# The sample's attention begun beside the prompt's output projection, in an encoder trunk of two batches on one core

## The chip, the cores and the metric

One core of a Trainium2 chip runs the whole program. Its engines are TensorE (PE, matrix products), VectorE (DVE), ScalarE (ACT), GpSimd (POOL) and SyncE (SP), which here issues nearly all transfers (DMAs). Each engine works through its own queue in order. The metric is the device time of one execution in microseconds, the median of several.

## The reference

A hybrid encoder layer is run for two batches with the same weights: `x_prompt` (512 rows) and `x_sample` (1024 rows), width 1024, all in float32.

```python
h = _rmsnorm(x, norm_attn_g)
z = h @ w_in                       # q 512 | k 128 | v 128 | ca 512 | cb 512
a_out = _window_attn(q, k, v, bias, band, attn_sink)   # 8 heads of 64, 2 kv heads, |q-k| <= 128
c = ca * jax.nn.sigmoid(cb)
c = _dwconv(c, conv_dw_w, conv_dw_b)                   # depthwise, 31 taps along the rows
c = jax.nn.silu(_layernorm(c, conv_ln_g, conv_ln_b))
x = x + jnp.concatenate([a_out, c], axis=-1) @ w_out
h = _rmsnorm(x, norm_ffn_g)
u = _dwconv(h @ w_up, ffn_dw_w, ffn_dw_b)              # 3 taps, 2 x 2816 channels
x = x + (jax.nn.silu(u[..., :D_FF]) * u[..., D_FF:]) @ w_down
return _rmsnorm(x, norm_final_g)
```

The attention scores get a bias per head from a table of relative positions (`bias`), and a sink logit per head.

## The kernel before

A product of two float32 matrices is made of three passes: each operand is split into a rounded part and the rest (`hi`, `lo`), and hi x hi, hi x lo and lo x hi are added up. `split` makes the parts: ACT rounds (L150), POOL or DVE subtracts (L151). One matmul is 128x128 weights by 512 columns.

The program goes in stages, in the order in which the code is written:

- **Projection A.** `order` lists the 14 column chunks of `w_in`. Each is split, multiplied (`proj`, L277 to L279) and evacuated (`evac`). The first four chunks are done for all three row tiles (the prompt, and two halves of the sample), the other ten for the prompt alone: `cs[0..3]` (the convolution's gates, cb and ca), `kv_`, then `qs` (four query chunks). Queries go to DRAM (`qsd`, L360) and come back per block (L551). The bias table is spread into DRAM (`bbd`), and `load_bias` fetches one 128x384 tile a head (L536).
- **Projection B beside the prompt's attention.** The ten chunks left for the sample: `kv_`, `cs[2]`, `qs`, `cs[3]`. Sample keys and values go to DRAM (`ksd` L377, `vsd` L393). At each `tick` in the projection, generators advance by a number of steps: `side` holds `prompt()`, that is, attention of 8 units (a unit is one block of 128 rows and one kv head) with the convolution's normalization (`conv_norm`: L675, L677 to L681, L687) for the last four.
- **Output projection of the prompt** (`out_half`, L711 to L713, weights L737 and L739), then `make_h2`, which scales the rows (L762, by the sum of squares that L723 makes) and transposes them (L237, L239, L240).
- **FFN of the prompt**, 22 steps (`ffn_step`): up projection, three taps (L846), gate (L864 to L869), down projection every second step (L884 to L887). Beside it runs `sample()`, from step `U0` = 3: attention of the sample's 16 units, loading and splitting of `w_out`, and two convolution norms. Keys, values and bias for it are loaded by `load_kv` (L749, L753) and a second `load_bias` just ahead.
- **The sample's output projection and FFN** (from L1039 on), which is ordered by hand and not touched.

A unit of attention: scores (`scores`, L574) into a PSUM bank, DVE adds the bias and takes the maximum (L578), ACT takes the exponential (L587), DVE the reciprocal (L589), ACT, DVE or POOL scale (L593, L595). Then transposes (L616), split (L618, L619), products with the values (L630, L631), evacuation (L638 to L642).

The depthwise convolution (`conv_items`) is not matrix work: 23 or 26 taps of a tile are multiply-adds on DVE (L313 first, L317 the others, accumulating in a PSUM bank, L325 last), 7 or 4 are products on ACT (L306, L309) added on POOL (L310). `convs` holds the prompt's four channel groups, `late` the sample's four. `pace` sets how much of each goes by at a tick: `rate` for `side`, `conv` for `convs`, `late` for `late` once `convs` is empty.

These steps give a written order only. A scheduler takes the instructions from it and fixes each engine's queue, and slots in SBUF (`sb`: 15 `q` of 4 KB, 61 `h` of 2 KB and others) and PSUM banks decide when a tile can be had; `use` says which banks a job may take.

## Time and profile before

| | |
|---|---|
| median of 3 runs | 1554.61 us (1553.9 to 1559.92) |
| profiled execution | 1557.32 us, its span 1555.2 us |
| TensorE (PE) | busy 1500.7 us, 96%, 6800 matmuls in the record |
| VectorE (DVE) | busy 1186.8 us, 76% |
| ScalarE (ACT) | busy 801.5 us, 52% |
| GpSimd (POOL) | busy 738.0 us, 47% |
| first score of the prompt | at 138 us |
| first output projection of the prompt | at 297 us |
| first transposing for its FFN | at 349 us |
| last down projection of the prompt | at 818 us |
| mean granted clock of TensorE | 0.987 |

The profile's page gives busy times, the span in 40 slices, and groups of instructions by line and engine. Its other views give busy times by stretch, with the granted clock of TensorE; the waits, each with the instruction that ended it (`PE a L574 <- DVE s L578: 6.5, 1, 6.5` says that the matmul of line 574 into a tile `a` waited for line 578 on DVE, 6.5 us in all, once, 6.5 at the longest); and the instructions in order of time. In the names of groups, `out<-in` are tiles by kind of slot (`h`, `q`, `c`, `d`; `a`, `b`, `c`, `u` are PSUM banks), and the two numbers behind the bar are the busy time and the mean ns of one. A queue's own entries are marked by a q (SPq).

### The profile page before, as it was taken

How to read it: one execution, taken by the hardware profiler on the slowest of the kernel's cores; microseconds unless marked ns; L12 is line 12 of the kernel's file. 1: busy time of each engine (PE TensorE's matmuls, PEld its weight loads, DVE VectorE, ACT ScalarE, POOL GpSimd, SP SyncE). 2: the span in 40 equal slices, each digit the busy share in tenths (PEclk: the TensorE clock that was granted, in tenths of full speed). 3: DMA queues.
4: the chain of work that ended last, by engine and by line, in shares of the span. 5: the costliest groups of instructions: out<-in, count | busy, mean ns of one | idle time of the engine just before them, and what ended most of it. 6: DMA issues, size and time to landing. Idle time of an engine off the chain costs nothing. (4 is left out here: it accounts for less than half of the span.)

```text
span 1555.2 us, 20044 instructions
## 1 busy us (share of the span) xinstructions
PE 1500.7 (96%) x6800; PEld 1232.1 (79%) x6800; DVE 1186.8 (76%) x1669; ACT 801.5 (52%) x1414; POOL 738.0 (47%) x648
## 2 busy tenths in 40 slices
PE   8998899897999999999999999999999999999997
PEld 7886688686877887888878888888888888788886
DVE  7787958656978899666665777877787877877795
ACT  7432654634566665555554454455444555544364
POOL 3464256226577776656562333555555554000135
PEclk9999899999999999999999999999999999999999
DMA  9435324634333333323547122332232232694642
GB/s 376 151 118 152 97 75 123 207 129 132 96 127 95 95 96 109 122 89 109 190 158 266 57 95 75 102 102 102 102 102 102 106 111 90 212 362 146 218 144 108
DMA packets 109441, 211.80 MB, mean 136 GB/s; under 512 B 11635, under 2 KB 33267, under 8 KB 109212
## 3 DMA queue, kind: packets, MB, share of 16 engines
q1 hardware_dynamic: 108092, 209.46, 40.4%
q8 instruction: 53, 0.87, 0.2%
q10 hardware_dynamic: 1248, 1.09, 0.2%
q14 instruction: 48, 0.39, 0.1%
HBM read 163.03 MB, written 48.51 MB: 136 GB/s over the span
## 5 line engine op out<-in xcount | busy, mean ns | idle before, releaser
L151 POOL TENSOR_TENSOR q<-q,q 128x1024 fp32r<-128x1024 f32 x66 | 159.0, 2412 | 88.7 <-ACT q L150 37.9
L992 POOL TENSOR_TENSOR q<-q,q 128x512 fp32r<-128x512 f32 x82 | 115.5, 1421 | 153.8 <-ACT q L1101 149.9
L277 PE MATMUL u<-h,q 128*128 128x512 f32 x384 | 151.4, 396 | 1.1 <-DVE h L846 0.7
L278 PE MATMUL u<-h,q 128*128 128x512 f32 x384 | 152.1, 396 | 0.0
L279 PE MATMUL u<-h,q 128*128 128x512 f32 x384 | 150.9, 393 | 0.0
L1115 PE MATMUL w<-h,q 128*128 128x512 f32 x372 | 146.2, 393 | 2.7 <-ACT h L1196 1.7
L1117 PE MATMUL w<-h,q 128*128 128x512 f32 x372 | 145.0, 390 | 0.7 <-POOL q L992 0.7
L317 DVE SCALAR_TENSOR_TENSOR c<-c,cvw,c 128x512 f32<-128x512 f32 x184 | 137.9, 750 | 2.5
L1116 PE MATMUL w<-h,q 128*128 128x512 f32 x350 | 136.2, 389 | 0.0
L150 ACT CAST q<-q 128x1024 fp32r<-128x1024 f32 x66 | 69.0, 1047 | 82.7 <-POOL q L151 39.9
L989 POOL TENSOR_TENSOR q<-q,q 128x1024 f32<-128x1024 f32 x8 | 23.8, 2994 | 180.7 <-DVE q L989 169.5
L1424 PE MATMUL w<-h,h 128*128 128x512 f32 x264 | 102.7, 389 | 0.0
L1426 PE MATMUL w<-h,h 128*128 128x512 f32 x264 | 102.7, 389 | 0.0
L992 DVE TENSOR_TENSOR h<-h,h 128x512 fp32r<-128x512 f32 (+1 forms) x128 | 92.2, 763 | 11.4 <-ACT h L996 9.5
L1425 PE MATMUL w<-h,h 128*128 128x512 f32 x244 | 94.9, 389 | 0.0
L992 POOL TENSOR_TENSOR c<-q,c 128x512 fp32r<-128x512 f32 x46 | 72.6, 1590 | 43.9 <-ACT c L1101 43.9
L996 ACT CAST h<-h 128x512 fp32r<-128x512 f32 x101 | 58.7, 619 | 58.4 <-DVE h L992 29.6
L1115 PEld LDWEIGHTS w<-h,q 128*128 128x128 f32 x372 | 69.8, 188 | 20.4 <-ACT w L1187 3.3
L277 PEld LDWEIGHTS u<-h,q 128*128 128x128 f32 x384 | 72.8, 190 | 16.3 <-DVE h L846 1.3
L279 PEld LDWEIGHTS u<-h,q 128*128 128x128 f32 x384 | 72.7, 189 | 14.2
L278 PEld LDWEIGHTS u<-h,q 128*128 128x128 f32 x384 | 72.7, 189 | 13.7
L1117 PEld LDWEIGHTS w<-h,q 128*128 128x128 f32 x372 | 69.8, 188 | 15.8 <-POOL q L992 1.1
(472 smaller groups left out, 4372.5 us busy)
## 6 DMA issues: line engine op xcount, KB each, us to landing
q<-in_laid_w_up SPq DMA_DIRECT2D x88, 512.0 KB, 3.6
h<-in_w_down SPq DMA_DIRECT2D x90, 256.0 KB, 4.2
ga<-q SPq DMA_DIRECT2D x64, 256.0 KB, 2.0
h<-ga SPq DMA_DIRECT2D x57, 256.0 KB, 3.8
q<-in_laid_w_in SPq DMA_DIRECT2D x22, 512.0 KB, 4.5
q<-in_x_sample SPq DMA_DIRECT2D x15, 512.0 KB, 7.6
h<-qsd SPq DMA_DIRECT2D x24, 256.0 KB, 3.1
q<-ga SPq DMA_DIRECT2D x20, 256.0 KB, 4.4
```

The lines of the kernel that those rows point to most:

```text
L151: (nc.vector if dve else nc.gpsimd).tensor_tensor(lo[:], raw[:], hi[:].bitcast(F32), op=ALU.subtract)
L277: nc.tensor.matmul(out, whi[:, kc, :], hi[:], start=(kc == 0), stop=False)
L278: nc.tensor.matmul(out, whi[:, kc, :], lo[:], start=False, stop=False)
L279: nc.tensor.matmul(out, wlo[:, kc, :], hi[:], start=False, stop=(kc == KC - 1))
L317: nc.vector.scalar_tensor_tensor(acc[:], src(t), w(t), acc[:], op0=ALU.mult, op1=ALU.add)
L992: (eng or nc.vector).tensor_tensor(out, a, b, op=ALU.subtract)
L1115: nc.tensor.matmul(out, whi[:, s], hi[:], start=(start and c == 0), stop=False, **go)
L1116: nc.tensor.matmul(out, whi[:, s], lo[:], start=False, stop=False, **go)
L1117: nc.tensor.matmul(out, wlo[:, s], hi[:], start=False, stop=(stop and c == 3), **go)
L1424: nc.tensor.matmul(out, sh[:, c], th[:], start=(p == 0), stop=False)
L1425: nc.tensor.matmul(out, sh[:, c], tl[:], start=False, stop=False)
L1426: nc.tensor.matmul(out, sl[:, c], th[:], start=False, stop=(p == NPAIR - 1))
```

## The change

The code moves work; it adds no computation, and TensorE's matmuls are the same in number.

- In projection A the prompt's keys, values and queries come right after `cs[0]` and `cs[1]`, and `cs[2]`, `cs[3]` last. Projection B has the order `kv_`, `qs`, `cs[2]`, `cs[3]`.
- The bias tiles for the prompt are loaded after chunk `BL` = 9 (the last queries), two heads to a slot of 4 KB (`q`), and not after projection A.
- The sample's convolution gets no share at the ticks of both projections (`late=0`). Once a tile of a convolution is begun it is finished before another queue goes on (`mid`).
- When the prompt's last scores are made (its bias list is empty), the sample's keys, values and bias are loaded, and the generator of its attention takes one step for each `SA` = 4 steps of the prompt's rest, output projection and `make_h2`. The rest of it runs in the FFN from step 0 instead of 3, at 0.44 steps a tick instead of 0.52; the loading of `w_out` for the sample waits for step `KW` = 21. Transposing in `make_h2` may use the banks `a` and `b`, before `a` alone.

```diff
-RA, RB, RBO, RD, RN, RE = 1.2, 0.8, 2.5, 0.52, 0.8, 0.9
+RA, RB, RBO, RD, RN, RE = 1.2, 0.8, 2.5, 0.44, 0.8, 0.9
-CL, CLO, CD = 0.5, 0.6, 0.65
+CLO, CD = 0.6, 0.65
-U0 = 3
+BL = 9
+SA = 4
+KW = 21
...
-    order = cs[0] + cs[1] + cs[2] + cs[3] + kv_ + qs
+    order = cs[0] + cs[1] + kv_ + qs + cs[2] + cs[3]
-    order += kv_ + cs[2] + qs + cs[3]
+    order += kv_ + qs + cs[2] + cs[3]
...
-        queue = convs or (late if pace["late"] else convs)
-        while queue and pace["credit"] > 0:
-            pace["credit"] -= advance(queue)
-        if not queue:
+        which = lambda: mid[0] if mid else convs or (late if pace["late"] else convs)
+        while which() and pace["credit"] > 0:
+            pace["credit"] -= advance(which())
+        if not which():
...
+    def load_bias(n):
+        b0 = bbd[:]
+        for h in range(0, NH, n):
+            bt = sb.tile([n, 3 * P])
+            for e in range(n):
+                nc.sync.dma_start(bt[:, e, :], bass.AP(...))
+                bias.append((bt, e))
-    pace.update(rate=RA, conv=CA, late=CL)
+    pace.update(rate=RA, conv=CA, late=0)
...
         if i == 2:
             bbd = bias_to_dram()
+        if i == BL:
+            load_bias(2)
...
-    pace.update(rate=RB, conv=CB, late=CL)
+    pace.update(rate=RB, conv=CB, late=0)
...
-    drain(side)
+    use.update(attn="a", norm="b", turn="ab")
+    while bias:
+        advance(side)
+    load_kv()
+    load_bias(1)
+    units_of_sample = attention(8, 24)
+    n = 0
+    while side:
+        advance(side)
+        n += 1
+        if n % SA == 0:
+            next(units_of_sample)
     drain(convs)
...
-    load_kv()
-    load_bias()
+    at = [0]
     def sample():
-        yield from attention(8, 24)
+        yield from units_of_sample
+        while at[0] < KW:
+            yield 0.0
...
     for k in range(NJ):
-        if k == U0:
+        at[0] = k
+        if k == 0:
             side.append(sample())
```

Lines of the changed file are numbered 2 to 22 higher: the score is L579, its reduction L583, a tap L321, the output projection L716 to L718, the transposing for the FFN L239, its scaling L767, a bias load L509.

How many instructions of some kinds stand in each stage of the order, before and after:

| stage | taps on DVE (L317) | score matmuls (L574) | products added on POOL (L310) | casts (L619) |
|---|---|---|---|---|
| up to the first score | 76, 60 | 0, 0 | 9, 9 | 0, 0 |
| to the first output projection | 74, 67 | 64, 64 | 13, 3 | 20, 18 |
| to the first transposing | 7, 0 | 0, 24 | 2, 0 | 0, 4 |
| to the last down projection | 131, 161 | 128, 104 | 36, 48 | 44, 42 |

Two score matmuls make one reduction (L578). First taps (L313) and last steps (L325) go from 5 and 6 to 7 and 8 in the last stage.

SP's queue around the bias loads. Before, they stand among the writes of the last queries (`qsd`) and of the sample's keys (`ksd`):

```order
L551 DMA h_220_1344<-qsd_153 128x512
L536 DMA h_215_1312<-bbd 128x384
L536 DMA h_216_1314<-bbd 128x384
L360 DMA qsd_153<-h_198_1234 64x4x128 x2
L536 DMA h_213_1308<-bbd 128x384
L536 DMA h_214_1310<-bbd 128x384
L327 DMA cvd_159<-h_161_958 128x512
L377 DMA ksd<-h_228_1396 64x512 x2
L377 DMA ksd<-h_229_1397 64x512 x2
L536 DMA h_209_1300<-bbd 128x384
L360 DMA qsd_153<-h_206_1289 64x4x128 x2
```

Now:

```order
L146 DMA q_179_1056<-in_laid_w_in 128x1024
L509 DMA q_187_1103<-bbd 128x384 x2
L509 DMA q_186_1100<-bbd 128x384
L509 DMA q_185_1097<-bbd 128x384 x2
L509 DMA q_186_1100<-bbd 128x384
L365 DMA qsd_153<-h_164_962 64x4x128 x2
L365 DMA qsd_153<-h_165_963 64x4x128 x2
L146 DMA q_189_1109<-in_laid_w_in 128x1024
L365 DMA qsd_153<-h_170_1005 64x4x128 x2
L365 DMA qsd_153<-h_171_1006 64x4x128 x2
L146 DMA q_193_1143<-in_laid_w_in 128x1024
L509 DMA q_188_1106<-bbd 128x384 x2
```

All eight loads have moved ahead of, or between, the writes of the prompt's queries, and two go into one `q` tile.

SP's queue ahead of the prompt's output projection, where the convolution's rows (`cvd`) are loaded for its norms. Before, the last two of them stand between the weights of the output projection (`in_w_out`):

```order
L737 DMA h_452_2838<-in_w_out 64x512 x2
L669 DMA h_445_2807<-cvd_159 128x4x128
L737 DMA h_453_2841<-in_w_out 64x512 x2
L737 DMA h_454_2844<-in_w_out 64x512
L737 DMA h_455_2847<-in_w_out 64x512 x2
L737 DMA h_482_3008<-in_w_out 64x512
L737 DMA h_479_2974<-in_w_out 64x512 x2
L737 DMA h_481_3005<-in_w_out 64x512
L669 DMA q_426_2673<-cvd_159 128x4x128
L737 DMA h_481_3005<-in_w_out 64x512
L737 DMA h_482_3008<-in_w_out 64x512
```

Now:

```order
L742 DMA h_438_2766<-in_w_out 64x512 x2
L744 DMA h_442_2775<-in_w_out 128x512
L758 DMA h_448_2790<-vsd 128x512
L509 DMA h_453_2801<-bbd 128x384
L509 DMA h_454_2803<-bbd 128x384
L509 DMA h_455_2805<-bbd 128x384
L509 DMA h_451_2797<-bbd 128x384
L509 DMA h_452_2799<-bbd 128x384
L509 DMA h_456_2807<-bbd 128x384
L509 DMA h_457_2809<-bbd 128x384
L674 DMA h_412_2607<-cvd_159 128x4x128
L509 DMA h_458_2811<-bbd 128x384
```

The load of `cvd` that is used last (`h_412`) has come to stand behind seven bias loads of the sample; `vsd` is a load of the sample's values.

TensorE's queue from that block's norm to the output projection. Before, the norm's transposes (L675, L687) stand behind the first output projection:

```order
L711 MATMUL u_128_2892<-h_474_2886,h_347_2186 128x512
L712 MATMUL u_128_2892<-h_475_2887,h_347_2186 128x512
L713 MATMUL u_128_2892<-h_474_2886,h_348_2187 128x512
L687 MATMUL a_121_2714<-ident,q_430_2695 128x128 x4
L675 MATMUL u_126_2809<-ident,h_445_2807 128x128 x4
L687 MATMUL a_127_2823<-ident,h_449_2821 128x128 x4
L711 MATMUL u_129_2920<-h_460_2858,h_280_1754 128x512
L712 MATMUL u_129_2920<-h_461_2859,h_280_1754 128x512
L713 MATMUL u_129_2920<-h_460_2858,d_281_1755 128x512
```

Now they stand ahead of it (L680, L692), and the sample's scores (L579) follow between its parts:

```order
L680 MATMUL u_118_2616<-ident,h_412_2607 128x128 x4
L635 MATMUL a_115_2566<-h_402_2544,h_159_919 128x512
L636 MATMUL a_115_2566<-h_403_2545,h_159_919 128x512
L635 MATMUL a_115_2566<-q_405_2562,h_159_919 128x512
L636 MATMUL a_115_2566<-q_406_2563,h_159_919 128x512
L621 MATMUL a_121_2675<-ident,h_394_2484 128x128
L621 MATMUL a_121_2675<-ident,h_395_2490 128x128
L621 MATMUL a_121_2675<-ident,h_398_2507 128x128
L621 MATMUL a_121_2675<-ident,h_399_2513 128x128
L692 MATMUL a_119_2642<-ident,h_416_2628 128x128 x4
L716 MATMUL u_128_2865<-h_459_2813,h_229_1421 128x512
L717 MATMUL u_128_2865<-h_460_2814,h_229_1421 128x512
```

```order
L717 MATMUL u_128_2865<-h_466_2826,h_229_1421 128x512
L718 MATMUL u_128_2865<-h_465_2825,h_230_1422 128x512
L716 MATMUL u_128_2865<-h_467_2829,h_347_2183 128x512
L635 MATMUL a_123_2699<-h_420_2680,h_160_922 128x512
L636 MATMUL a_123_2699<-h_421_2681,h_160_922 128x512
L579 MATMUL a_127_2857<-q_443_2777,h_475_2845 128x256
L579 MATMUL a_127_2857<-q_444_2778,h_475_2845 128x256
L579 MATMUL a_126_2851<-q_443_2777,h_475_2845 128x256
L579 MATMUL a_126_2851<-q_444_2778,h_475_2845 128x256
L579 MATMUL a_132_2944<-q_445_2783,h_476_2847 128x256
```

The last norm (`u_118`, `a_119`) has moved ahead of the first output matmul, and score matmuls of the sample into it.

TensorE's queue at the end of the prompt's output projection. Before, the transposes (L237) of its rows (`q_512` to `q_515`) follow:

```order
L712 MATMUL u_135_3147<-h_503_3051,h_443_2805 128x512
L713 MATMUL u_135_3147<-h_502_3050,h_444_2806 128x512
L237 MATMUL a_136_3186<-ident,q_512_3178 128x128
L237 MATMUL a_136_3186<-ident,q_513_3180 128x128
L237 MATMUL a_137_3195<-ident,q_512_3178 128x128
L237 MATMUL a_137_3195<-ident,q_513_3180 128x128
L237 MATMUL a_138_3204<-ident,q_512_3178 128x128
L237 MATMUL a_138_3204<-ident,q_513_3180 128x128
L237 MATMUL a_136_3186<-ident,q_514_3182 128x128
L237 MATMUL a_137_3195<-ident,q_514_3182 128x128
L237 MATMUL a_138_3204<-ident,q_514_3182 128x128
```

Now (L239, rows `q_541` to `q_544`):

```order
L718 MATMUL u_146_3225<-h_522_3102,h_427_2725 128x512
L239 MATMUL b_149_3285<-ident,q_541_3277 128x128
L239 MATMUL b_149_3285<-ident,q_542_3279 128x128
L239 MATMUL b_150_3294<-ident,q_541_3277 128x128
L239 MATMUL b_150_3294<-ident,q_542_3279 128x128
L239 MATMUL a_151_3303<-ident,q_541_3277 128x128
L239 MATMUL a_151_3303<-ident,q_542_3279 128x128
L621 MATMUL a_152_3312<-ident,h_488_2947 128x128
L621 MATMUL a_152_3312<-ident,h_489_2953 128x128
L621 MATMUL a_152_3312<-ident,h_491_2987 128x128
L621 MATMUL a_152_3312<-ident,h_492_2993 128x128
L239 MATMUL a_153_3321<-ident,q_541_3277 128x128
```

Four transposes of a sample unit (L621) have come between them.

More of the change, by code (lines that the diff above doesn't have):

```diff
@@ L243, in transposed @@
             yield 0.0
+    mid = []
     side, pace = deque(), dict(rate=0.0, due=0.0, conv=0.0, credit=0.0, late=0.0)
@@ L270, in drain @@
         while queue:
-            advance(queue)
+            advance(mid[0] if mid else queue)
     def proj(out, w, h):
@@ L310, in offload @@
                     nc.gpsimd.tensor_tensor(pacc[:], pacc[:], pr[:], op=ALU.add)
+            mid.append((convs, late)[g])
             acc = bank("conv")
@@ L495, in bias_to_dram @@
         return d
-    pace.update(rate=RA, conv=CA, late=CL)
+    bias = []
+    def load_bias(n):
[3 more added lines that the diff above has]
+            for e in range(n):
+                nc.sync.dma_start(bt[:, e, :], bass.AP(b0.tensor, b0.offset + (h + e) * NT + P - 1, [[NH * NT - 1, P], [1, 3 * P]]))
+                bias.append((bt, e))
+    pace.update(rate=RA, conv=CA, late=0)
     NALL = 4
@@ L529, in tile_hybrid_encoder @@
     rbs.pop(0)
-    bias = []
-    b0 = bbd[:]
-    def load_bias():
-        for h in range(NH):
-            bt = sb.tile([3 * P])
-            nc.sync.dma_start(bt[:], bass.AP(b0.tensor, b0.offset + h * NT + P - 1, [[NH * NT - 1, P], [1, 3 * P]]))
-            bias.append(bt)
-    load_bias()
     blocks = [(G, b) for G in GR for b in range(G["nb"])]
@@ L578, in scores @@
             nc.vector.tensor_tensor_reduce(
-                out=p[:, :nk], in0=sc[:, :nk], in1=bias[h][:, off:off + nk], scale=-1.0,
+                out=p[:, :nk], in0=sc[:, :nk], in1=bias[h][0][:, bias[h][1], off:off + nk], scale=-1.0,
                 scalar=nsink[:, h:h + 1], op0=ALU.add, op1=ALU.min, accum_out=negm[:, j:j + 1])
@@ L771, in prompt @@
         yield from attention(0, 8, {u: conv_norm(u - 4) for u in range(4, 8)})
-        kt.clear(), vt.clear(), qt.clear(), bias.clear()
+        for kv in range(NKV):
+            kt.pop((0, kv))
+        vt.pop(0)
+        bias.clear()
         pace.update(rate=RBO, late=CLO)
@@ L943, in ffn_end @@
         down(G, parts, fin)
-    use.update(attn="a")
+    use.update(norm="au", turn="a")
     for half in range(2):
```

2 lines of the change are left out of this document (1 added, 1 removed).

## The prediction

> **What bounds the kernel now.** I read the page first, then the busy time by stage, then who TensorE waited for, then the timeline at each of those waits.
>
> ```profile
> span 1555.2 us, 20044 instructions
> PE 1500.7 (96%) x6800; PEld 1232.1 (79%) x6800; DVE 1186.8 (76%) x1669; ACT 801.5 (52%) x1414; POOL 738.0 (47%) x648
> PE   8998899897999999999999999999999999999997
> PEclk9999899999999999999999999999999999999999
> ```
>
> TensorE (PE) is busy 96% of the span, and the order shows the same matrix work after the change. So only its gaps and its slow clock can be gained. Apart from the first and the last slice, PE's dips (slices of 39 us) and the clock's one 8 lie between 117 and 389 us. The stages: 138 is the first score of the prompt, 297 its first output projection, 349 the transposing for its feed-forward network (FFN), 380 to 820 the FFN with the sample's attention beside it.
>
> ```profile
> core 0: us, PE busy (x) PEld busy (x) DVE busy (x) ACT busy (x) POOL busy (x), PEclk, DMA share, GB/s
> 138.00:180.00 42.00, 31.02 (x128) 24.73 (x129) 35.77 (x72) 18.13 (x46) 13.12 (x17) 0.84 0.46 136
> 180.00:297.00 117.00, 113.14 (x546) 94.08 (x545) 81.91 (x153) 65.94 (x135) 55.20 (x58) 0.99 0.38 106
> 297.00:349.00 52.00, 47.26 (x205) 38.05 (x204) 30.76 (x45) 19.95 (x37) 13.77 (x16) 0.97 0.50 170
> 349.00:380.00 31.00, 22.57 (x108) 17.82 (x107) 21.68 (x28) 15.89 (x24) 18.92 (x15) 0.89 0.52 150
> 380.00:540.00 160.00, 157.63 (x724) 129.27 (x723) 135.57 (x235) 93.86 (x170) 110.68 (x94) 1.00 0.33 101
> 540.00:700.00 160.00, 156.95 (x729) 129.03 (x728) 128.74 (x223) 96.56 (x180) 109.11 (x95) 0.99 0.32 106
> 700.00:820.00 120.00, 116.21 (x539) 95.33 (x538) 80.65 (x128) 66.46 (x131) 72.09 (x68) 0.99 0.49 158
> ```
>
> What a stage loses is its PE idle time plus the missing clock over its busy time. For 138 to 180: 42.00 - 31.02 = 11.0, and 0.16 x 31.0 = 5.0, together 16.0. In the same way 3.9 + 1.1 = 5.0, then 4.7 + 1.4 = 6.1, then 8.4 + 2.5 = 10.9, 2.4, 3.1 + 1.6 = 4.7, and 3.8 + 1.2 = 5.0. In all 50 us: no order of this work can gain more there. TensorE's waits in 138 to 380:
>
> ```profile
> PE a L574 <- DVE s L578: 6.5, 1, 6.5
> PE a L237 <- DVE q L762: 5.5, 1, 5.5
> PE b L277 <- DVE q L339: 3.4, 1, 3.4
> PE a L687 <- DVE h L681: 2.9, 1, 2.9
> PE a L574 <- DMA q<-ksd: 2.6, 2, 2.0
> PE a L687 <- DVE q L681: 1.3, 1, 1.3
> PE a L630 <- ACT h L618: 1.2, 1, 1.2
> PE u L631 <- DVE h L619: 1.1, 1, 1.1
> PE u L616 <- DVE h L640: 0.8, 1, 0.8
> PE u L630 <- ACT h L618: 0.6, 1, 0.6
> ```
>
> **The change, term by term.** First, the start of the prompt's attention. The longest wait is a score for a PSUM bank, which VectorE (DVE) frees only when the bias tile of that head has landed:
>
> ```profile
> 152.45 0.81 SPq L536 DMA_DIRECT2D h<-bbd  x2
> 153.93 0.52 SPq L536 DMA_DIRECT2D h<-bbd  x1
> 157.31 0.48 DVE L578 CUSTOM_DVE_ANT_0 h<-a,h,nsink 128x256 f32<-128x256 f32 x1 [0.76 <-DMA h<-bbd]
> 158.26 0.76 PE L574 MATMUL a<-h,h 128*128 128x256 f32 x2 [6.47 <-DVE s L578]
> ```
>
> The last bias loads are issued at 152 to 154, among the writes of the last queries and the sample's keys, and the DVE row at 157 still ends a wait for one. In the changed order six of the eight stand ahead of the query writes and two among them, and those queries are four weight chunks older when the attention starts. So this wait goes, and most of the slow clock behind it. DVE also has less to do there: by the order 67 convolution taps instead of 74 between first score and output projection, and 60 instead of 76 before. Next in line are the links inside an attention unit (the last four rows, 1.2 + 1.1 + 0.8 + 0.6, about 4); I let them stay. I take 16.0 - 4.0 = 12 gained. Ends: 6.5, the bias wait alone, and 16.
>
> Second, 180 to 349, with 11.1 lost. Moved into the output projection are 24 score matmuls (12 reductions by L578) and a few values. This is work of later stages, so it gains only what it fills. The 3.4 wait on L339 begins on ScalarE (ACT), which held DVE up:
>
> ```profile
> 278.22 1.93 SPq L739 DMA_DIRECT2D h<-in_w_out  x4
> 286.24 0.62 ACT L150 CAST h<-h 128x512 fp32r<-128x512 f32 x1 [5.92 <-DMA h<-in_w_out]
> 300.37 4.78 SPq L536 DMA_DIRECT2D h<-bbd  x4
> 326.66 1.75 SPq L753 DMA_DIRECT2D h<-vsd  x4
> ```
>
> ACT sat 5.92 us for w_out, with its other work queued behind. After the change SP has seven of the sample's bias loads ahead of the last load of convolution rows (cvd), and the norm made from these now stands in TensorE's queue ahead of the first output matmul. At 1.75 / 4 = 0.44 to 4.78 / 4 = 1.2 us an issue, seven are 3 to 8 us; before, bias and values came at 300 and 327 by these two rows, after the weights. The eight ksd loads also move ahead, beside projections, where SP has time. In favour, the scores stand between the output matmuls, where the norms' two waits (L681, 2.9 + 1.3) are now; half of that is 2. I take 2 gained. Ends: 11 gained, and 8 lost.
>
> Third, 349 to 380, with 10.9 lost. The ksd wait (2.6) goes, since kt is loaded before. The wait on L762 stays: the chain from the last output matmul through L716, L723, L134, L135 to L762 is the same, and in it the new order has four transposes only.
>
> ```profile
> 349.13 1.32 PE L237 MATMUL a<-ident,q 128*128 128x128 f32 x9
> 355.93 0.90 PE L237 MATMUL a<-ident,q 128*128 128x128 f32 x3 [5.47 <-DVE q L762]
> ```
>
> Four at 1.32 / 9 = 0.15 cover 0.6 of the 5.47. I take 2.6 + 0.6, 3 gained; ends 0 and 9. The Trainium skill, page "TensorE: Matmul & The Clock Gate", section "HAM oscillation — how this bites in real kernels", says that idle gaps over about 3.4 us bring the half clock back. The trace agrees (clock 0.89 around this gap); by the rule the 2.5 of slow clock stay with the gap, and the sum is the same.
>
> Fourth, the FFN, 380 to 820, with 12.1 lost. What it gets and gives, with the costs of 375 to 800:
>
> ```profile
> L317 DVE SCALAR_TENSOR_TENSOR c<-c,cvw,c 128x512 f32<-128x512 f32 x115 | 86.1, 749 | 1.4
> L310 POOL TENSOR_TENSOR h<-h,h 128x512 f32<-128x512 f32 x30 | 39.9, 1329 | 2.6 <-ACT h L309 1.4 <-ACT h L306 0.5
> L578 DVE CUSTOM_DVE_ANT_0 h<-a,h,nsink 128x384 f32<-128x384 f32 (+1 forms) x64 | 36.3, 578 | 25.4 <-PE a L574 12.7 <-DMA catd<-h 3.9 <-PE a L631 3.8
> L865 DVE SCALAR_TENSOR_TENSOR h<-h,h 128x512 f32<-128x512 f32 x22 | 32.4, 1472 | 7.7 <-ACT h L864 6.8 <-POOL h L151 0.8
> L619 DVE TENSOR_TENSOR h<-a,h 128x512 fp32r<-128x512 f32 x42 | 28.5, 684 | 13.3 <-ACT h L618 12.0 <-POOL h L151 1.0
> L151 POOL TENSOR_TENSOR q<-q,q 128x1024 fp32r<-128x1024 f32 x41 | 99.1, 2418 | 36.9 <-PE u L279 22.2 <-issue 5.8 <-ACT h L618 2.9
> ```
>
> By the counts DVE gets 30 taps (22.5 us) and two first and last steps each (about 3), and gives 12 reductions (6.9), and two casts (1.4): +17. POOL gets 12 additions: +16. From 380 to 700 DVE goes from 135.6 + 128.7 = 264 to 281 of 320, 83% to 88%. If the 7.1 lost there grows as DVE's free time shrinks, it becomes 7.1 x 56 / 39 = 10.2, so 3 lost. Against it, attention starts at step 0 and not 3 and goes at 0.44 a tick instead of 0.52, so the steps in which taps and attention meet are 15% lighter in attention: its 36.3 + 28.5 of these two rows alone give 9.7 less in the crowded part, more than half of the 17. I take 0; ends 4 gained, 9 lost. The sample's output weights wait for the last step (KW); they came about there before, so 0.
>
> Sum: 12 + 2 + 3 + 0 = 17. The profiled execution took 1557.32, its span and 2.1 around it, and 2.7 more than the median of the runs, 1554.61. So 1557.3 - 17 = 1540.3 for its like, and 1537.6, rounded 1538, for the median. Differences under 0.5% (8 us) can't be told from none.
>
> **Rivals.** (A) The scores fill the output projection as they are meant to: the second term at 9 and the third at 7 instead of 2 and 3. 1554.6 - 28 = 1527. For it: DVE is only 30.76 of 52 busy there. Against it: TensorE takes its queue in order, so a score whose operands are late makes a gap and doesn't fill one.
>
> (B) The first output projection waits for the last norm, whose rows SP loads behind seven bias tiles. The 8 lost replace the 2: 12 - 8 + 3 = 7, 1548, within 0.5%. For it: the 5.92 that ACT waited here for DMAs already, and the order. Against it: at 0.44 us an issue it is 3.
>
> (C) Slower: the FFN's weights come late from POOL. Each step needs two splits of 2418 ns on POOL, in order, and the 12 additions that wait for ACT's products now stand among them; POOL is 69% busy (110.68 of 160) and goes to 74%. It decides from 25 us, that is 25 / 21 = 1.2 us late in each step; with 1.9 us a step, 40 - 17 = 23 worse, 1578. Against it: of TensorE's waits in 375 to 820, POOL ends none; the longest are these.
>
> ```profile
> PE b L884 <- DVE q L887: 2.1, 4, 0.6
> PE a L574 <- DMA q<-ksd: 2.0, 1, 2.0
> ```
>
> (D) POOL's additions hold DVE up. L865, with both inputs in SBUF, takes 1472 ns in the FFN, where L619, with one in PSUM, takes 684; POOL works on SBUF beside both. If each of the 12 additions holds DVE for its 1329 ns and all of it reaches TensorE, 17 - 16 = 1 is left, 1554. Against it: the taps, most of DVE's work, have one input in PSUM and take 749. The Trainium skill, page "SBUF — State Buffer", section "SBUF: two separate sides", says it as a rule: a VectorE instruction with two SBUF inputs and a GpSimd instruction that reads SBUF shut each other out. The 1472 agrees with it.
>
> **How the numbers follow.** The forecast has 0.46 (gains of 10 to 22), A 0.22, B 0.15, C 0.06, D 0.05; 0.06 is for what I don't see. Faster takes the forecast, A, half of that rest and a fifth of B, whose 7 is near the line: 0.74. Same takes the other four fifths of B and D, 0.17. Slower takes C and the other half of the rest, 0.09. The ends of the terms give -6.5 + 8 + 0 + 9 = 10 worse to 16 + 11 + 9 + 4 = 40 better. The range reaches to A, with 5 us more for its own spread, and to B's end, where the start gains the bias wait alone: 1522 to 1555.
>
> **What would show it.** Right: no wait of L579 (the score) for DVE over 2 us near 138 to 175, and clock 0.95 or more in that stage; no wait for ksd; a wait on L767 (L762 now) of 4 to 6 us still there; the 471 from the first transposing to the last down projection (349 to 820) now 463 to 473. Wrong: a wait over 3 us for the last norm's rows or its L686 just before the first output matmul (B); TensorE waiting for POOL's L153 splits, step after step (C); no gap over 2 us between 250 and 350 (A). The forecast falls with the first term: if another wait takes the bias wait's place, most of the gain is gone.

## The result, and the profile after

The changed kernel takes 1532.9 us (median of 4 runs, 1530.2 to 1536.0) against 1556.6 for the kernel before on the same chip (4 runs, 1553.9 to 1559.9): ratio 0.9847, 95% interval 0.9818 to 0.9877, or 23.7 us less. The forecast was 1538 with a range of 1522 to 1555. The total came out close; its four terms, as the stages show, mostly did not.

The page after, against the first fence of the prediction (busy time, then TensorE and its clock in 40 slices, now of 38 us):

```profile
span 1531.3 us, 20070 instructions
PE 1494.0 (98%) x6800; PEld 1227.9 (80%) x6800; DVE 1179.4 (77%) x1669; ACT 800.9 (52%) x1414; POOL 739.6 (48%) x648
PE   8999999799999999999999999999999999999997
PEclk9999999899999999999999999999999999999999
```

One dip is left between the first and the last slice, the eighth (268 to 306 us). The busy time by stage, with edges at the same events as in the prediction (first score 135, first output matmul 292.6, first transposing 345.2, last down projection 787; the FFN in one row, then 80 us of what follows):

```profile
core 0: us, PE busy (x) PEld busy (x) DVE busy (x) ACT busy (x) POOL busy (x), PEclk, DMA share, GB/s
135.10:177.10 42.00, 40.60 (x206) 33.88 (x205) 39.91 (x86) 26.57 (x65) 14.32 (x18) 1.00 0.33 105
177.10:292.60 115.50, 103.73 (x486) 84.30 (x484) 69.92 (x132) 51.96 (x109) 42.45 (x54) 0.94 0.55 153
292.60:345.20 52.60, 51.06 (x234) 41.96 (x233) 27.81 (x62) 28.00 (x64) 12.47 (x21) 1.00 0.23 75
345.20:376.20 31.00, 28.99 (x143) 23.35 (x142) 22.71 (x39) 24.87 (x44) 26.13 (x21) 0.94 0.39 112
376.20:787.00 410.80, 407.08 (x1882) 335.43 (x1881) 350.43 (x568) 241.97 (x432) 298.60 (x244) 1.00 0.38 121
787.00:867.00 80.00, 79.47 (x387) 65.54 (x387) 53.32 (x79) 34.55 (x73) 20.71 (x35) 1.00 0.47 164
```

Loss is again TensorE's idle time plus the missing clock over its busy time: for the second row 115.50 - 103.73 = 11.8 and 0.06 x 103.7 = 6.2, together 18.0. The same six rows were read for every kernel below. A clock rounded to 0.01 leaves the FFN row uncertain by about 2 us (0.005 x 410); by one such row the FFN before lost 13.5 (12.1 by the prediction's three). The experiments ran in three groups (e1 to e4, e5 to e8, e9 to e12), each with runs of the kernel before beside it (medians 1557.2, 1555.1 and 1555.9), and the ratios are to those.

| kernel | median us | ratio to before (95%) | first 42 us | to first output matmul | output projection | turning, 31 us | FFN | 80 us behind |
|---|---|---|---|---|---|---|---|---|
| before | 1556.6 | 1 | 15.9 | 5.0 | 6.2 | 10.9 | 13.5 | 0.0 |
| changed | 1532.9 | 0.985 (0.982 to 0.988) | 1.4 | 18.0 | 1.5 | 3.7 | 3.7 | 0.5 |
| e1 no early units | 1565.5 | 1.006 (1.004 to 1.008) | 1.2 | 19.8 | 2.2 | 14.8 | 20.2 | 0.0 |
| e2 convolution free | 1560.2 | 1.002 (1.001 to 1.004) | 2.5 | 34.5 | 4.8 | 4.9 | 5.5 | 0.3 |
| e3 old order | 1543.0 | 0.991 (0.989 to 0.993) | 17.3 | 1.4 | 16.7 | 4.6 | 3.9 | 0.3 |
| e4 later loads | 1553.0 | 0.998 (0.996 to 0.999) | 1.3 | 15.2 | 2.6 | 8.8 | 19.3 | 0.0 |
| e5 RB 1.0 | 1575.1 | 1.013 (1.010 to 1.015) | 3.5 | 17.5 | 25.1 | 9.6 | 4.9 | 6.1 |
| e6 RB 0.9 | 1557.2 | 1.002 (1.000 to 1.004) | 1.2 | 13.3 | 13.7 | 8.3 | 8.0 | 7.0 |
| e7 SA 6 | 1552.8 | 0.998 (0.996 to 1.000) | 1.3 | 15.9 | 1.2 | 13.9 | 15.1 | 1.5 |
| e8 RD 0.52 | 1549.4 | 0.996 (0.994 to 0.998) | 1.2 | 18.5 | 1.6 | 2.8 | 8.7 | 7.8 |
| e9 one piece of w_out | 1528.5 | 0.982 (0.980 to 0.984) | 5.9 | 7.9 | 2.1 | 2.4 | 4.9 | 0.4 |
| e10 banks a alone | 1550.4 | 0.996 (0.995 to 0.997) | 1.4 | 17.6 | 3.2 | 9.3 | 10.3 | 0.6 |
| e11 RD 0.40 | 1546.3 | 0.994 (0.992 to 0.996) | 1.4 | 19.0 | 1.6 | 3.0 | 9.0 | 5.0 |
| e12 SA 3 | 1551.6 | 0.997 (0.996 to 0.999) | 1.4 | 17.3 | 5.1 | 9.6 | 12.7 | 0.4 |

The changed kernel wins 14.5 in the first 42 us, gives back 13.0 before the first output matmul, and wins 4.7, 7.2 and 9.8 behind it: 22.7 with the last column, of 23.9 by which the span is shorter. TensorE's waits between 177 and 350, against the list in the prediction (the first 42 us have none over 0.7):

```profile
PE u L680 <- DMA h<-cvd: 3.2, 1, 3.2
PE b L680 <- DMA h<-cvd: 2.8, 1, 2.8
PE u L621 <- ACT h L598: 2.4, 1, 2.4
PE a L636 <- DVE h L624: 1.7, 2, 1.1
PE a L239 <- DVE h L624: 1.4, 1, 1.4
```

The 6.5 for the bias tile, the 5.5 on the scaled rows and the wait for `ksd` are gone. New are two waits for convolution rows. What lies around them, from the timeline (PE, ACT, DVE and SP's queue; L282 is the projection's last matmul, L583 a reduction of the scores, L592 an exponential of the attention, L716 the first output matmul):

```profile
264.20 0.50 ACT L592 ACTIVATE h<-h,s 128x257 f32<-128x257 f32 x1
...
266.60 4.68 SPq L742 DMA_DIRECT2D h<-in_w_out  x4
...
273.58 0.62 ACT L152 CAST h<-h 128x512 fp32r<-128x512 f32 x1 [8.80 <-DMA h<-in_w_out]
...
274.81 0.40 PE L282 MATMUL b<-h,q 128*128 128x512 f32 x1
276.54 1.45 DVE L153 TENSOR_TENSOR h<-h,h 128x512 fp32r<-128x512 f32 x2 [5.69 <-ACT h L152]
277.05 4.36 SPq L509 DMA_DIRECT2D h<-bbd  x7
277.97 0.67 PE L680 MATMUL b<-ident,h 128*128 128x128 f32 x4 [2.77 <-DMA h<-cvd]
277.90 0.48 DVE L583 CUSTOM_DVE_ANT_0 h<-a,q,nsink 128x256 f32<-128x256 f32 x1
279.50 0.51 ACT L592 ACTIVATE h<-h,s 128x257 f32<-128x257 f32 x1
281.61 0.56 SPq L674 DMA_DIRECT2D h<-cvd  x1
287.77 1.11 PE L680 MATMUL u<-ident,h 128*128 128x128 f32 x4 [3.19 <-DMA h<-cvd]
292.55 0.48 PE L716 MATMUL u<-h,h 128*128 128x512 f32 x1
```

ACT sits 8.8 us ahead of the first split of `w_out`, until the weights land. DVE waits 5.69 for ACT's split, and the last reduction of the prompt's attention (277.90) stands behind that in DVE's queue. So the attention's last exponential (279.50) comes 15 us after the one before it, and 5.2 after its scores, which TensorE makes at 274.26. In the kernel before, all 32 exponentials of the prompt are done ahead of ACT's wait for these weights (5.92 us, until 286.24); the last is this one:

```profile
274.64 0.51 ACT L587 ACTIVATE q<-q,s 128x257 f32<-128x257 f32 x1
```

In the changed kernel the projections have run out at 274.8, and until the first output matmul TensorE is busy less than half of the time, at a low clock (the last three numbers of a row are clock, DMA share and GB/s):

```profile
275.20:292.50 17.30, 8.06 (x32) 5.82 (x32) 10.33 (x20) 11.56 (x26) 3.71 (x9) 0.61 0.82 234
```

Two explanations stand there side by side: the wait for the weights of the output projection, and SP's seven bias tiles ahead of the last convolution rows (the prediction's B).

### The profile page after: what moved, and what is told of

Its sections match the earlier page's. It is cut to its first block, busy times and chain, and to the rows that moved or that the text cites. A ratio compares the mean times of both kernels' runs of the same rounds, so it can differ in the third digit from the quotient of the medians.

```text
span 1531.3 us, 20070 instructions
## 1 busy us (share of the span) xinstructions
PE 1494.0 (98%) x6800; PEld 1227.9 (80%) x6800; DVE 1179.4 (77%) x1669; ACT 800.9 (52%) x1414; POOL 739.6 (48%) x648
## 5 line engine op out<-in xcount | busy, mean ns | idle before, releaser
L282 PE MATMUL u<-h,q 128*128 128x512 f32 x384 | 150.2, 391 | 0.1
L321 DVE SCALAR_TENSOR_TENSOR c<-c,cvw,c 128x512 f32<-128x512 f32 x184 | 137.7, 748 | 1.8
L1011 POOL TENSOR_TENSOR q<-q,q 128x1024 f32<-128x1024 f32 x8 | 23.9, 3001 | 182.1 <-DVE q L1011 169.9
L313 POOL TENSOR_TENSOR h<-h,h 128x512 f32<-128x512 f32 x57 | 76.0, 1333 | 31.4 <-ACT h L312 29.3
L1137 PEld LDWEIGHTS w<-h,q 128*128 128x128 f32 x372 | 70.0, 188 | 20.5 <-ACT w L1209 3.6
L280 PEld LDWEIGHTS u<-h,q 128*128 128x128 f32 x384 | 72.2, 188 | 17.0 <-DVE h L865 2.1
L282 PEld LDWEIGHTS u<-h,q 128*128 128x128 f32 x384 | 72.1, 188 | 15.1 <-POOL q L153 0.5
L153 POOL TENSOR_TENSOR h<-h,h 128x512 fp32r<-128x512 f32 x52 | 70.3, 1356 | 28.9 <-ACT h L152 20.8
```

Of the source, the lines that this page charges most:

```text
L153: (nc.vector if dve else nc.gpsimd).tensor_tensor(lo[:], raw[:], hi[:].bitcast(F32), op=ALU.subtract)
L280: nc.tensor.matmul(out, whi[:, kc, :], hi[:], start=(kc == 0), stop=False)
L282: nc.tensor.matmul(out, wlo[:, kc, :], hi[:], start=False, stop=(kc == KC - 1))
L321: nc.vector.scalar_tensor_tensor(acc[:], src(t), w(t), acc[:], op0=ALU.mult, op1=ALU.add)
L1137: nc.tensor.matmul(out, whi[:, s], hi[:], start=(start and c == 0), stop=False, **go)
```

## The experiments

**Which part earns what: e1 to e4.**

e1:

```diff
-RA, RB, RBO, RD, RN, RE = 1.2, 0.8, 2.5, 0.44, 0.8, 0.9
+RA, RB, RBO, RD, RN, RE = 1.2, 0.8, 2.5, 0.52, 0.8, 0.9
-KW = 21
+KW = 0
...
-    use.update(attn="a", norm="b", turn="ab")
+    use.update()
     while bias:
         advance(side)
-    load_kv()
-    load_bias(1)
     units_of_sample = attention(8, 24)
-    n = 0
-    while side:
-        advance(side)
-        n += 1
-        if n % SA == 0:
-            next(units_of_sample)
+    drain(side)
...
-    use.update(norm="au", turn="a")
+    use.update(attn="a", turn="a")
...
+    load_kv()
+    load_bias(1)
     at = [0]
...
-        if k == 0:
+        if k == 3:
```

> The changed kernel without the early start of the sample's attention: its keys, values and bias are loaded at the start of the FFN and its attention goes from step 3 at 0.52 a tick, as before. Projection order, early bias and held convolution stay. Loss is TensorE's idle time plus the missing clock over its busy time; changed kernel: 1.4 (first score to 42 us later), 18.0 (from there to the first output matmul), 1.5 (output projection), 3.7 (turning), 3.7 (FFN). Theory: the sample's loads on SP cost the boundary, and the early units pay in turning and FFN. Then the boundary falls to about 5 (13 gained), output projection, turning and FFN go back to 6, 11 and 12 or more (20 lost): 1533 + 7 = 1540, up to 1546 as the held taps now meet all the attention. Rival: the FFN's gain is from the held convolution or the freed banks, not from the early units: FFN stays near 4, boundary falls, 1522 to 1530.

Measured: 1565.5. The rows of the stage before the first output matmul, the turning and the FFN:

```profile
177.20:296.90 119.70, 106.31 (x488) 85.07 (x486) 76.92 (x139) 56.99 (x117) 48.61 (x51) 0.94 0.47 138
343.40:374.40 31.00, 20.29 (x90) 15.90 (x88) 20.87 (x33) 12.21 (x21) 12.10 (x12) 0.80 0.43 112
374.40:828.00 453.60, 437.81 (x2005) 358.61 (x2005) 370.23 (x616) 265.43 (x493) 306.61 (x268) 0.99 0.36 117
```

The loss before the first output matmul is 19.8, though the sample's loads no longer stand ahead of the weights: the loss comes without them, and half of the theory falls. The other half holds, and was too small: without early units turning and FFN lose 35.0, against 7.4 in the changed kernel and 24.4 before. (Banks and rates went back with them, so the 27.6 are not the units' alone.)

e2:

```diff
-pace.update(rate=RA, conv=CA, late=0)
+pace.update(rate=RA, conv=CA, late=0.5)
-pace.update(rate=RB, conv=CB, late=0)
+pace.update(rate=RB, conv=CB, late=0.5)
```

> The changed kernel with the sample's convolution no longer held: it may run beside the projections at 0.5 a tick, as before. Theory: the first stage was won by the bias tiles and the projection order, so its loss stays under 4 (from 1.4), the FFN gets some 20 to 30 taps fewer, and the time is 1528 to 1535. Rival: the first stage was won because DVE had fewer taps beside the prompt's attention: with the taps back the loss there is 6 to 12, and the time 1538 to 1545.

Measured: 1560.2, so both times were wrong. The first 42 us stay won (2.5), as the theory said, and the price comes behind them, where DVE has 90.0 us of work instead of 69.9 and its results come late:

```profile
179.30:306.90 127.60, 104.64 (x484) 85.11 (x482) 90.00 (x161) 57.63 (x119) 51.01 (x63) 0.89 0.51 144
PE u L579 <- DVE h L645: 5.5, 1, 5.5
```

Holding the sample's convolution back is worth 27 us, 16.5 of it in that stage. Without it the change would not be faster than before.

e3:

```diff
-    order = cs[0] + cs[1] + kv_ + qs + cs[2] + cs[3]
+    order = cs[0] + cs[1] + cs[2] + cs[3] + kv_ + qs
-    order += kv_ + qs + cs[2] + cs[3]
+    order += kv_ + cs[2] + qs + cs[3]
-        if i == BL:
-            load_bias(2)
     drain(side)
     h1.pop(0)
     rbs.pop(0)
+    load_bias(1)
```

> The changed kernel with the projections in their old order (the prompt's keys, values and queries last) and the prompt's bias tiles loaded after them, one by one; held convolution and early sample attention stay. Theory: the wait of the score for a bank, held by a reduction that waits for its bias tile, comes back with its slow clock: loss of the first stage 10 to 16 instead of 1.4, time 1542 to 1550. Rival: the held convolution alone had freed DVE and so the stage: loss under 5, time 1531 to 1537.

Measured: 1543.0, as the theory said, but not where:

```profile
138.00:180.00 42.00, 30.85 (x123) 24.51 (x123) 35.45 (x72) 18.23 (x46) 13.15 (x17) 0.80 0.47 140
180.00:294.60 114.60, 113.22 (x556) 94.39 (x555) 64.08 (x126) 57.48 (x122) 43.52 (x53) 1.00 0.41 117
294.60:358.80 64.20, 53.42 (x238) 43.29 (x237) 29.86 (x66) 28.92 (x66) 10.89 (x22) 0.89 0.54 149
PE a L578 <- DVE s L582: 6.6, 1, 6.6
PE a L578 <- DMA q<-ksd: 9.6, 2, 9.2
```

The bias wait is back (6.6; loss 17.3), but the next stage then loses 1.4: both stages together 18.7, against 19.4 in the changed kernel and 20.9 before. So the new order and the early bias tiles moved a loss and removed next to none of it up to there. What they are worth (10 us in all) shows in the output projection, which loses 15.2 more without them, 9.6 of it a wait for the sample's keys: the old order can't feed the early units.

e4:

```diff
-    load_kv()
-    load_bias(1)
...
         n += 1
-        if n % SA == 0:
+        if n == 24:
+            load_kv()
+            load_bias(1)
+        if n >= 24 and n % SA == 0:
             next(units_of_sample)
```

> The changed kernel with the sample's keys, values and bias tiles asked for 24 pulls of the side work later, so that on SP the last convolution rows and most of the first output weights stand ahead of all eight bias tiles; the sample's scores begin with them. Theory: the boundary's loss of 18 was these loads in the way of w_out and of the convolution rows; it falls to 6 to 10, the later stages lose 0 to 4 of what they had won, and the time is 1524 to 1530. Rival: the boundary's loss is the values and norms themselves, or w_out comes late for want of free slots: loss stays at 15 to 18, time 1531 to 1537.

Measured: 1553.0. The stage before the first output matmul loses 15.2, as the rival said, and the FFN pays 15.6 more, which neither had:

```profile
372.60:811.40 438.80, 423.70 (x1924) 344.57 (x1923) 361.58 (x588) 251.78 (x450) 307.37 (x255) 0.99 0.36 115
```

With the last convolution rows ahead of all eight bias tiles the gain there is 18.0 - 15.2 = 3. But this order does not bring the rows sooner: SP issues the last of them at 281.60 (281.61 in the changed kernel), now behind loads of `w_out`. So the bias tiles aren't the main cause, and among what is left are the weights. Two units of the sample are early instead of three, and the FFN loses 19.3.

**The loss before the first output matmul: e5, e6, e9.**

e5 and e6:

```diff
-RA, RB, RBO, RD, RN, RE = 1.2, 0.8, 2.5, 0.44, 0.8, 0.9
+RA, RB, RBO, RD, RN, RE = 1.2, 1.0, 2.5, 0.44, 0.8, 0.9
```

(0.9 in e6.)

> The changed kernel with RB 1.0 instead of 0.8: at each tick of projection B the prompt's attention takes a quarter more steps, so that in the order no transposes and values are left between the last projection and the first output matmul (34 matmuls there in the changed kernel, 18 us for 2.5 us of work); the output projection begins among the last projections. Theory: the 15 won at the start were given back because the attention's tail then stood alone behind the projections; with the tail covered the loss from first score to first output matmul falls from 19 to 5 to 9, and the time to 1519 to 1525. Rival: the attention goes no faster than DVE lets it (95% busy in the first 42 us), so the wait only moves into the projections: loss there 15 or more, time 1530 to 1536.

> The changed kernel with RB 0.9: in the order 5 score matmuls of the sample stand between last projection and first output matmul instead of the 34 matmuls of units and norms, and 15 instead of 29 scores of the sample stand in the output projection. Theory (tail alone): loss from first score to first output matmul 6 to 10 instead of 19; since only half as many sample units are early, the turning and FFN lose 10 to 19 more, as in the kernel with later loads: 1530 to 1542. Rival (the early units do not matter to the FFN): 1520 to 1526.

Measured: 1575.1 and 1557.2, above everything that was expected of either. The tail is covered (in e5 the projections go on to 335 us, in e6 0.5 us lie between the last and the first output matmul), and still 17.5 and 13.3 are lost; the first output matmul comes at 292.2 and 289.9, as if nothing had changed, and the output projection then loses 25.1 and 13.7. Covering the tail only moved the loss. (The 18 us that e5's text gives 2.5 us of work hold 8.1 in the profile, as the row 275.20 to 292.50 shows.) SP's waits in e5 show what is late next:

```profile
SPq L141 <- PE b L282: 14.5, 1, 14.5
```

A load of the prompt's rows waits 14.5 us for a slot that the projection's matmuls give back, and the convolution rows, the weights and the bias tiles stand behind it in SP's queue. More attention beside the projections leaves the projections, and their slots, later.

e9:

```diff
+            if n == 0:
+                wor.update({(kc, 0): piece[0] for kc in range(KC)})
+                piece.clear()
...
+    piece = [sb.tile([NT])]
+    nc.sync.dma_start(piece[0][:], w_out[0, 4 * P:5 * P, :NT])
     side.append(prompt())
```

> The changed kernel without the loads of the first half of the prompt's output weights: one 128x512 piece, loaded before projection B, stands for all eight (their splits on ACT, POOL and DVE and all matmuls stay). In the changed kernel ACT sat 8.8 us behind the first of these loads, with an exponential and the norms queued behind. Theory: this wait in ACT's queue holds the attention's last units back while the projections run out, so without it the loss from first score to first output matmul falls from 19.4 to 8 to 12 and the time to 1522 to 1527. Rival (SP's bias tiles ahead of the convolution's rows; by this order two loads of rows stand behind seven tiles): loss 16 to 20, time 1530 to 1536.

Measured: 1528.5. This kernel leaves out seven of the eight pieces of that half, so it is a probe and no version to use. ACT no longer waits for `w_out` between 250 and 300 (10.8 in three waits in the changed kernel), and TensorE's two waits for convolution rows are 1.6 and 1.0 instead of 2.8 and 3.2:

```profile
ACT h L152 <- DMA h<-in_w_out: 10.8, 3, 8.8
...
PE b L680 <- DMA h<-cvd: 1.6, 1, 1.6
PE u L680 <- DMA h<-cvd: 1.0, 1, 1.0
135.20:177.20 42.00, 39.23 (x185) 32.49 (x185) 39.09 (x84) 22.25 (x57) 12.69 (x17) 0.92 0.35 107
177.20:288.20 111.00, 106.31 (x507) 87.40 (x506) 72.70 (x136) 55.87 (x119) 45.17 (x56) 0.97 0.50 145
```

(The first row is the changed kernel's, the others are e9's, its first two stages last.) The stage loses 7.9 instead of 18.0, with SP's bias tiles still ahead of the rows. So the weights' loads are the larger part of what was given back in this stage, 10.1 of 13.0. By which path is not separated. Without them ACT and DVE wait for no such split, and the attention's last exponential comes 1.7 us after its scores (271.69 and 270.02) and not 5.2; SP also has twelve loads fewer to issue, and the last convolution rows are issued at 276.57 instead of 281.61. The sum of both stages, 13.8, lies above the theory's 8 to 12 and below the rival's 16 to 20: over both stages only 5.6 are won, because the first 42 us now lose 5.9 instead of 1.4; 0.08 x 39.2 = 3.1 of that is slow clock, and why it came is open. The total is 4.4 us less between medians, and the intervals of the ratios overlap: the stage shows a cause, the total doesn't prove its size.

**Turning and FFN: e7, e8, e10, e11, e12.** Each changes one number of the changed kernel:

```diff
-SA = 4
+SA = 6
```

in e7 (3 in e12), `RD` 0.52 instead of 0.44 in e8 (0.40 in e11), and in e10

```diff
-    use.update(attn="a", norm="b", turn="ab")
+    use.update(attn="a", norm="b", turn="a")
```

> The changed kernel with one step of the sample's attention for each 6 instead of 4 steps of the prompt's rest: 19 instead of 29 of the sample's scores stand in the output projection, all else of that stage is the same. The kernel with later loads had 18 there and lost 27 instead of 7 in turning and FFN, and 22 without any. Theory (each early unit takes a unit from the crowded FFN): turning and FFN lose 20 to 28, time 1546 to 1554. Rival (the later loads themselves, or the fit of that order, made the loss): turning and FFN lose 7 to 12, time 1532 to 1538.

> The changed kernel with the sample's attention in the FFN at the old 0.52 steps a tick instead of 0.44; the early units and the start at step 0 stay. Theory (the slower rate thins the attention where taps meet it): loss of the FFN 8 to 14 instead of 3.7, time 1537 to 1543. Rival (only the early units count): 3 to 5, time 1531 to 1535.

> The changed kernel with the transposing for the FFN kept to the three banks a, as before, instead of a and b. The wait of 5.5 on the scaled rows was forecast to stay and came to 1.4 on another line. Theory (two more banks let transposes run ahead of the late rows): the wait comes back at 3 to 6 and the turning loses 7 to 11 instead of 3.7: 1537 to 1541. Rival (the units of the sample between the transposes cover it): turning 3 to 5, time 1531 to 1535.

> The changed kernel with the sample's attention in the FFN at 0.40 steps a tick instead of 0.44 (0.52 gave 16 more). Theory (the lighter each step, the less is lost): loss of the FFN 2 to 4, time 1527 to 1533. Rival (0.44 is just enough for the attention to be done before step 21, and below it the sample's output weights and norms come late): the last third of the FFN and the 80 us behind it lose 5 to 12 more: 1537 to 1545.

> The changed kernel with one step of the sample's attention for each 3 instead of 4 steps of the prompt's rest: still 29 scores in the order of the output projection, 16 transposes instead of 8. Theory (an early unit is worth more than the room it takes; 6 instead of 4 steps cost 20): turning and FFN lose 5 to 7 instead of 7.4 and the output projection 1 to 3: 1528 to 1533. Rival (what 4 has done is an order that happens to fit, and another order fits worse whichever way it goes): turning and FFN lose 12 to 25, 1538 to 1552.

Measured: 1552.8, 1549.4, 1550.4, 1546.3 and 1551.6. Fewer early units are worse, and so are more; a faster rate is worse, and so is a slower one. Their FFN rows, in the order e7, e8, e10, e11, e12, against 3.7 lost in the changed kernel:

```profile
373.80:813.50 439.70, 428.90 (x1960) 352.26 (x1960) 362.32 (x583) 254.54 (x457) 310.20 (x252) 0.99 0.37 119
377.30:806.00 428.70, 419.97 (x1925) 344.04 (x1924) 356.46 (x582) 248.15 (x443) 301.63 (x247) 1.00 0.37 121
378.30:805.00 426.70, 416.38 (x1913) 342.58 (x1912) 354.58 (x570) 247.48 (x443) 305.31 (x249) 1.00 0.36 117
378.50:800.80 422.30, 413.27 (x1906) 339.78 (x1905) 355.36 (x571) 245.21 (x435) 302.28 (x245) 1.00 0.37 119
382.40:808.60 426.20, 417.69 (x1903) 341.14 (x1902) 361.57 (x574) 244.02 (x434) 304.25 (x243) 0.99 0.37 119
```

e7 bore out its theory (29.0 in turning and FFN, 1 above its end), e8 its theory's FFN (8.7, and 7.8 more behind it, that nobody had), e10 its theory's turning, with an FFN that loses 6.6 more and so a time 9 above the forecast. e11 and e12, one step to the other side, came out about as the rivals said and take the ground from a slope of load. So 0.44 and 4 don't stand on such a slope: both sides of them are higher. The order of TensorE's queue fits this. Of its first 3600 instructions from the first transposing on, e9 and e3 keep over 99.8% in the changed kernel's sequence; they lose 7.7 and 8.8 from the turning to the 80 us behind (the last three columns), the changed kernel 7.9. In e4 to e8 and e10 to e12 the scheduler dealt them anew (82 to 89% can still be found in the same sequence), and these eight lose 17.0 to 30.5 there, 22.7 in the mean, about what the kernel before lost (24.4). Each of the eight has its own number changed as well, so that the order is the cause is argued, not shown; that eight changes in both directions all cost 9 to 23 us there is measured. Against it stands e2: its order is as new (89%), and it loses only 10.7 there. It has fewer convolution taps left for the FFN (104 on DVE instead of 154, which is 75% busy in place of 85%). So a new order alone does not bring the loss; it would have to be an order that meets a busy DVE, and that is not tried.

e10 asks for the banks' part. The wait on the scaled rows is back, at 3.7 of 5.5, and the turning loses 9.3. But it is also there in e5 and e6, which have the banks `a` and `b` (the three rows are e10, e5, e6):

```profile
PE a L239 <- DVE q L767: 3.7, 1, 3.7
PE b L239 <- DVE q L767: 4.8, 1, 4.8
PE b L239 <- DVE q L767: 4.6, 1, 4.6
```

So two more banks don't end the wait by themselves. In e12, with these banks and a wait of 0.3, the turning still loses 9.6.

## Why the prediction was right, and where it wasn't

That the time was in range is luck: two errors met. The gain of the first term was given back, and turning and FFN gave 17.0 where the terms had 3. Most of the change's neighbours don't have these 14.

- **First term (12 gained, at the start).** Right at its place: no wait of L579 for DVE, clock 1.00, 14.5 gained. Wrong as a gain of the kernel: 13.0 came back in the next stage, and e3, with the bias wait restored, loses no more over both (18.7 against 19.4). The step that failed is what was named as late next, the links inside a unit. What came late were the weights of the output projection: without their loads that stage loses 10.1 less (e9). ACT waits for them, and DVE for ACT: the wait of 5.92 that the second term quoted as a fact of the kernel before grew to 8.80, since ACT comes to that split 15.5 us sooner than before (264.8 against 280.3) and the weights only 12.7 (273.6 against 286.2). And now an exponential of the prompt's attention stands behind it, where before all were done.
- **Second term (2 gained; ends 11 gained, 8 lost).** 8.3 lost (5.0 + 6.2 against 18.0 + 1.5). Rival B named this size and this place, and what would show it came true, a wait of 3.2 for the last norm's rows. Its mechanism had the smaller part: with no sample loads at all the loss is 19.8 (e1), with the rows ahead of the tiles 15.2 (e4), without the weights' loads 7.9 (e9). A wait that ends on the forecast instruction was not proof of the forecast reason.
- **Third term (3 gained).** 7.2. The `ksd` wait went as forecast. "The wait on L762 stays" was wrong: 1.4 was left, on another line. The chain behind the rows is the same, but the transposes may use two more banks and the sample's units stand between them; without the banks the wait is 3.7 and the turning loses 9.3 (e10). That the banks carry these 5.6 of the 7.2 is not shown, as e5 and e6 have them and wait 4.8 and 4.6. The change of `use` was in the diff and got no price.
- **Fourth term (0; ends 4 gained, 9 lost).** 9.8 gained by one row, outside its ends. The stretch from the first transposing to the last down projection, forecast at 463 to 473, is 441.8 (345.2 to 787.0): 17.0 of the difference to 469.5 before (349.1 to 818.6) is loss that is gone, the rest is mostly work that now stands ahead of it. For the turning and the FFN of such a change as a rule the forecast of 3 was fair: the held taps cost (35.0 in e1 against 24.4 before), the early units pay them back, and the eight other orders end at 22.7 against 24.4. The changed kernel's own 7.9 is 15 less than their mean, and e2, e3 and e9 (10.7, 8.8, 7.7) are near it. The model behind the end of 9 lost, that loss grows as DVE's free time shrinks, is not borne out by these two kernels: DVE is busier in the FFN than before (350.43 of 410.80, 85%; before 135.57 + 128.74 + 80.65 of 440, 78%), and the loss is smaller.
- **Rival A** gave 1527, nearer in total than B, for a reason that did not happen: the output projection was filled (loss 1.5), but the stage before lost more than that. Its 7 for the third term is what was measured. **C and D** did not come: POOL ends no wait of TensorE between 177 and 820, and the FFN is faster with the 12 additions in it. Of DVE's instructions with both inputs in SBUF the gate's first (L865, now L884) takes 1372 ns in the FFN instead of 1426, the one behind it (L866, now L885) 1071 instead of 770, 4.8 us in all; TensorE doesn't show them as lost.

Shown are that the start's gain was given back (e3), that the held convolution, the early sample keys and the early units with their banks and rates are each needed (e2, e3, e1), and that the loads of the output projection's weights have a part in what was given back, 10.1 in their stage and 5.6 over both (e9). Open are the path of that loss, the banks' part, and why the changed kernel loses so little in the FFN: no single wait was found that explains 15 us.

## What to carry to other kernels

When a wait at the start of a stage is removed, follow the stage to its end and ask what arrives late there: the weights moved up by 12.7 us and ACT's need of them by 15.5, and ACT and DVE, which take their queues in order, held the attention behind them. Where a scheduler deals the queues, one number changed by a step can cost more than the mechanism that it was meant for: try its neighbours on both sides before a gain is credited to the idea. The five neighbours with one number changed (e7, e8, e10 to e12) stand at 1546 to 1553, ratios 0.994 to 0.998: 3 to 9 us of the change's 23.7 are left there. As far as these five tell, the rest belongs to this one setting.

## What the runs showed of the hardware

The half clock came in gaps shorter than the prediction's rule. In the traces the granted clock changes only at steps of 3.41 us: in the changed kernel it is 0.5 from 278.43 to 292.08 (four steps) and from 350.11 to 353.52 (one). TensorE's last wide matmul before the first fall is at 274.81; then only transposes run until 288.5 (L680, L621, L692), between waits of 2.77, 2.37 and 3.19. In the step before the fall, which holds the first of these waits, TensorE is busy for 0.64 of 3.41 us. Before the second fall no wait is over 1.42, and only transposes run:

```profile
346.70:350.10 3.40, 1.72 (x12) 1.00 (x10) 1.35 (x2) 2.21 (x5) 2.39 (x3) 1.00 0.00 0
350.10:353.50 3.40, 3.21 (x12) 2.52 (x13) 3.23 (x5) 3.04 (x6) 3.16 (x4) 0.50 0.00 0
```

The Trainium skill, page "TensorE: Matmul & The Clock Gate", section "Part 4: PE-mode transpose", says that transposes don't count as busy for the clock in the same way. These two places would fit that, but e11's trace does not: in one step there are 16 transposes and nothing else, with the same longest wait of 1.42, and the clock stays full in the next step. Here the measurement decides.

```profile
348.32:351.73 3.41, 1.88 (x16) 1.40 (x15) 1.46 (x3) 2.38 (x5) 1.69 (x3) 1.00 0.00 0
351.73:355.14 3.41, 2.77 (x19) 1.92 (x17) 2.53 (x4) 3.25 (x6) 3.25 (x3) 1.00 0.00 0
```

e8 and e9 have such a step too (16 and 18 transposes, busy 55% and 59%). What parts the cases is TensorE's busy share of the step, transposes counted like any matmul: 1.72 of 3.40 (51%) lost the clock, 1.88 of 3.41 (55%) kept it. Over the steps at full clock between 30 and 1515 us in all 14 traces, the clock fell after each of the 40 with a share under 40%, after 20 of the 58 between 40 and 62%, and after none of the 5869 above. So here a stretch is to be priced by how busy TensorE is in 3.41 us, and not by its longest gap or by what kind of matmul runs. No run tries this by itself.
